# The output layer of the Hyena filters: two fp32 matmuls over 64 rows, or single passes with a low part in the other 64 rows

## The chip, the cores and the metric

The kernel runs on one core of a Trainium2 chip. Its time is device microseconds for one execution; the median of three runs counts. Beside these times there is one profiled execution, from which every line of the profile below is taken. PE is the matmul engine (its weight loads are listed apart, as PEld), DVE the vector engine, ACT the scalar engine, POOL the GpSimd engine, SP the engine whose queue issues most of the transfers (DMA).

## The reference, cut to what matters

The program is one layer of a bidirectional encoder over 2048 positions of width 1024: an input projection, a Hyena group (long convolutions by FFT), an mLSTM group, an output projection, cross-attention and an MLP. The change lies in the Hyena group's filters. They are generated, not stored: a small network with two sine layers of 64 units runs over position features, a linear output layer makes 2048 channels of it (2 orders x 2 directions x 512), a window damps them, and the spectrum is taken.

```
z = concat([t, cos(bands * ang), -sin(bands * ang)])          # (2048, 33)
hid = sin(fr1 * (z @ w1 + b1))                                # (2048, 64)
hid = sin(fr2 * (hid @ w2 + b2))
filt = (hid @ w3).reshape(L, 2, 2, 512)                       # order, direction, channel
filt = filt * exp(-t * abs(deltas))
two_sided = concat([filt[:, :, 0], 0, flip(filt[1:, :, 1])])
spec = rfft(two_sided)
```

Everything is fp32, and the result is held to it.

## The kernel before

The whole layer is one stream of instructions per engine. Python generators emit the work; `weave` interleaves two of them in the ratio of the weights that it is given, by the numbers that they yield. `filters()` (L158) is woven with the first sweeps of the input projection: `weave(p.filters(), s, 230, 200)` (L1621). The tile framework then orders the instructions of each engine with a timeline simulation of its own (`schedule_with_timeline_sim`, L1581, the planner in what follows), inserts the waits, and gives out buffers: a tile of a given tag takes one of that tag's `bufs` slots and waits until the tile that had it is done with. An engine then takes its queue strictly in that order; an instruction that waits holds up all behind it.

`filters()` has three parts.

The sine layers (L201 to L213) make `hid`, 128 rows x 2048 positions: the upper 64 rows are the hidden units at position t, the lower 64 the same units at the mirrored position, for the backward direction. The weights `w1` and `w2` hold two copies on the diagonal, so one matmul serves both directions. They, the biases and the output weights `w3` come over POOL's queue (L175 to L187) at the very start of the program, beside the loads of x and of the projection's weights over SP's queue.

The taps loop (L244 to L263) runs over 16 residues j of the position modulo 16 (two per iteration, `j2` and `jj`) and two orders o. Each of these 32 steps multiplies every 16th column of `hid` by `w3`: L253 takes the upper 64 rows (forward), L254 the lower 64 (backward), each one fp32 matmul, which the profile shows as two records. DVE multiplies both by the window (L256, L257), adds them (L261), POOL subtracts them (L262). One step late, `front` (L235) multiplies sum and difference by the 128 x 128 matrix `f1` (L238, fp32), ACT copies the result into the tile `st` (L239), and after the second residue SP stores it to `fs` in memory (L241). A window tile holds two residues of one direction (512 KB); `windows` (L219) loads the next two ahead.

The blocks loop (L265 to L286) runs over 32 blocks, 16 for each order: SP loads a block of `fs` (L270) and two matrices `dm` (L268), PE multiplies (L284, fp32, two matmuls), ACT copies (L285), SP stores to `hd` (L286). `hyena()` reads `hd` later: L663 and L664, each a half of 64 rows, every half loaded to two places. The loads run two blocks ahead.

All tiles of the three parts come from one pool, `f_sb`: seven tiles of tag `a` (128 x 2 x 512, 512 KB), used for windows, `st`, and the loads and results of the blocks loop, and eight of tag `b` (128 x 512).

In the projection's sweeps (L295 to L297), a product of two fp32 operands is already made of three single passes in the type fp32r: each operand is split into a rounded high part (ACT, L300) and the remainder (DVE, L301), and high x high, low x high and high x low are summed. `natural()` (L593) makes the projection's columns that aren't convolved; its result goes through a tile `so` (L614) to memory, beside `st` tiles of a tag with three buffers that `prep_norm` and `sweep_out` use.

Of the kernel before, what the change touches and what calls it, by code (L numbers as in the profile page):

```python
# [18 lines left out]
L = 2048  # L19
D = 1024  # L20
CH = 512
# [6 lines left out]
def shape_constants():  # L28
# [13 lines left out]
    winb = win[back].copy()  # L42
    winb[0] = 0.0
    c_win = np.stack([win, winb], 0)

# [22 lines left out]
    dm = np.zeros((32, 2, 64, 2, 64))  # L68
# [29 lines left out]
class Prog:  # L98
# [59 lines left out]
    def filters(self):  # L158
        nc, tc, a = self.nc, self.tc, self.a
        sd = [self.dram(f"fs{o}", (2, 128, 16, CH)) for o in range(2)]  # L160
        hd = self.dram("hd", (2, 32, 128, CH))
        with tc.tile_pool(name="f_sb", bufs=1, side="right") as sb:
            def ta(bufs=7):
                return sb.tile([128, 2, CH], F32, tag="a", name="a", bufs=bufs)

            def tb(bufs=8):
                return sb.tile([128, CH], F32, tag="b", name="b", bufs=bufs)

            w1 = sb.tile([66, 128], F32, name="w1")
            w2 = sb.tile([128, 128], F32, name="w2")  # L170
            w3 = sb.tile([128, 2, CH], F32, name="w3")
            f1 = sb.tile([128, 2, 128], F32, name="f1")
            nc.vector.memset(w1, 0.0)
            nc.vector.memset(w2, 0.0)
            nc.gpsimd.dma_start(out=w1[0:33, 0:64], in_=a["hy_filt_w1"][0])  # L175
# [8 lines left out]
            w3v = a["hy_filt_w3"][0].rearrange("k (o r c) -> r k o c", o=2, r=2)  # L184
            for h in range(2):
                nc.gpsimd.dma_start(out=w3[64 * h:64 * h + 64], in_=w3v[h])
            nc.gpsimd.dma_start(out=f1, in_=a["c_f1"])  # L187
# [12 lines left out]

            hid = sb.tile([128, L], F32, name="hid")  # L201
# [12 lines left out]

            skip, skip2 = tb(), tb()
            for o, t in enumerate((skip, skip2)):
                nc.scalar.dma_start(out=t[0:1], in_=a["hy_skip"][:, o])
            wv = a["c_win"].rearrange("r (q j) c -> r q j c", j=16)
            def windows(j2):  # L219
                if j2 == 8:  # L220
                    return None
                w = ta(), ta()
                for r in range(2):
                    nc.sync.dma_start(out=w[r], in_=wv[r, :, 2 * j2:2 * j2 + 2])
                return w
# [17 lines left out]
            nxt = windows(0)  # L243
            for j2 in range(8):  # L244
                js = slice(2 * j2, 2 * j2 + 2)
                yield 14
                (wf, wb), nxt = nxt, windows(j2 + 1)
                for o in range(2):
                    st = [ta() for p in range(2)]
                    for jj in range(2):  # L250
                        j = 2 * j2 + jj
                        pf, pb = self.hy(), self.hy()
                        nc.tensor.matmul(pf, hid[0:64, j::16], w3[0:64, o], start=True, stop=True)  # L253
                        nc.tensor.matmul(pb, hid[64:128, j::16], w3[64:128, o], start=True, stop=True)  # L254
                        f, b = tb(), tb()
                        nc.vector.tensor_tensor(f, pf, wf[:, jj], ALU.mult)  # L256
                        nc.vector.tensor_tensor(b, pb, wb[:, jj], ALU.mult)  # L257
                        if j == 0:
                            nc.vector.tensor_tensor(f[0:1], f[0:1], (skip, skip2)[o][0:1], ALU.add)
                        e = [tb() for p in range(2)]  # L260
                        nc.vector.tensor_tensor(e[0], f, b, ALU.add)  # L261
                        nc.gpsimd.tensor_tensor(e[1], f, b, ALU.subtract)  # L262
                        late(lambda e=e, st=st, jj=jj, o=o, js=js: front(e, st, jj, o, js))  # L263
            late(None)
            def blocks(o, i):  # L265
                p, k = divmod(2 * i, 16)
                dm = sb.tile([128, 2, 128], F32, tag="dm", name="dm", bufs=3)
                nc.sync.dma_start(out=dm, in_=a["c_dm"][:, 2 * i:2 * i + 2])  # L268
                t = ta()
                nc.sync.dma_start(out=t, in_=sd[o][p, 8 * k:8 * k + 16].rearrange("(k r) j c -> (r j) k c", k=2))  # L270
                return dm, t
# [3 lines left out]
            for n, (o, i) in enumerate(order):  # L275
                if True:
                    yield 3.4
                    dm, t = q.pop(0)
                    if n + 2 < 32:
                        q.append(blocks(*order[n + 2]))  # L280
                    hs = ta()
                    for m in range(2):
                        pp = self.hy()
                        nc.tensor.matmul(pp, dm[:, m], t[:, m], start=True, stop=True)  # L284
                        nc.scalar.copy(hs[:, m], pp)  # L285
                    nc.sync.dma_start(out=hd[o, 2 * i:2 * i + 2].rearrange("k l c -> l k c"), in_=hs)  # L286

# [305 lines left out]
    def natural(self, hf, tiles, after=None):  # L593
# [3 lines left out]
        for c2 in tiles:  # L597
# [3 lines left out]
            for t in range(8):  # L601
# [24 lines left out]
    def hyena(self, es):  # L626
        nc, tc, a = self.nc, self.tc, self.a
        hy = self.dram("hy", (3, L, CH)).rearrange("s (q j) c -> s q j c", j=16)
        hd = self.dram("hd", (2, 32, 128, CH))
        yh = self.dram("yh", (L, CH)).rearrange("(q j) c -> q j c", j=16)  # L630
# [22 lines left out]
        def load2(o, i):  # L653
# [6 lines left out]
            nc.sync.dma_start(out=t, in_=sds[o][p, 8 * k:8 * k + 16].rearrange("(k r) j c -> (r j) k c", k=2))  # L660
            src = hd[o, 2 * i:2 * i + 2].rearrange("k (r l) c -> r l k c", r=2)
            for h in range(2):
                nc.sync.dma_start(out=hr[64 * h:64 * h + 64], in_=src[0])  # L663
                nc.sync.dma_start(out=hi[64 * h:64 * h + 64], in_=src[1])  # L664
            if i == 0:
                nc.sync.dma_start(out=hr[64:65, 0], in_=hd[o, 0, 64:65])
                nc.vector.memset(hi[0:1, 0], 0.0)
                nc.vector.memset(hi[64:65, 0], 0.0)
# [943 lines left out]
def program(p):  # L1612
    with ExitStack() as ms:
        with ExitStack() as es:
# [5 lines left out]
            next(s)  # L1620
            weave(p.filters(), s, 230, 200)  # L1621
            p.flush()
# [53 lines left out]
```

## Time and profile before

| | us |
|---|---|
| median of three runs | 3380.28 |
| the three runs | 3380.11, 3380.28, 3384.89 |
| the profiled execution | 3389.34 |
| its span | 3387.6 |
| PE busy in the span | 3200.0 |
| DVE, ACT, POOL busy | 2084.2, 1459.1, 1227.3 |

The table is read as follows. The span is the stretch between the first and the last instruction on the chip; the execution's own time has 1.7 us around it. Busy time of PE counts a matmul from its start to its modelled end, and matmuls overlap, so the distance from one start to the next is the better price. A line of the profile names the source line, engine, operation, output tile and input tiles; `x64` is the number of instructions, three numbers with slashes are the shortest, median and longest duration in ns, and brackets hold the idle time ahead of an instruction and what ended it. On the timeline, the first number is the start and the second the duration, in us.

The filters' parts are found by the first and last starts of their lines: the sine layers' first matmul (L208) is at 29.8, the last sine (L199) at 110.4; the taps loop's matmuls (L253) run from 112.9 to 300.9, the last `front` to 309.6; the blocks loop (L284) from 313.9 to 461.5.

### The profile page before, as it was taken

Reading aid. Unit: us, or ns where it says so; the run is one execution under the profiler, and the core shown is the slowest. Engines: PE = TensorE matmul, PEld = TensorE weight load, DVE = VectorE, ACT = ScalarE, POOL = GpSimd, SP = SyncE. Lnnn points to the kernel's source line nnn. Section 1 sums busy time; section 2 is a strip of 40 time slices with the busy share of each in tenths; the row PEclk is TensorE's granted clock in tenths of the full one; section 3 lists DMA queues with packets and bytes.
Section 4 is the critical chain, followed back from the end, with each engine's and each line's share of the span. In section 5 each row is a group of like instructions: output and inputs, shape, how many; then the busy total and the mean of one; then the engine's idle time right before and its main releaser. Section 6 shows DMA issues by size and latency. Waiting matters only on the chain.

```text
span 3387.6 us, 46777 instructions
## 1 busy us (share of the span) xinstructions
PE 3200.0 (94%) x15671; PEld 2560.6 (76%) x15671; DVE 2084.2 (62%) x3855; ACT 1459.1 (43%) x2771; POOL 1227.3 (36%) x862
## 2 busy tenths in 40 slices
PE   6999999899899988799999999999999999999997
PEld 5656666577676877688897987788788887888876
DVE  7584324443556757787776554765854576556695
ACT  4344434442554233344344444555655543333335
POOL 2131001210122312333325012876766564434482
PEclk9999999899999989899999999999999999999998
DMA  5356888996999578856547444765654475444424
GB/s 164 115 205 206 277 288 232 258 322 254 253 242 296 178 236 277 256 162 215 187 152 265 144 134 155 224 206 184 199 171 157 148 242 174 128 140 140 128 94 159
DMA packets 480750, 674.55 MB, mean 199 GB/s; under 512 B 41739, under 2 KB 256849, under 8 KB 479485
## 3 DMA queue, kind: packets, MB, share of 16 engines
q1 hardware_dynamic: 478904, 668.70, 62.4%
q0 software_dynamic: 1600, 2.86, 0.3%
q8 instruction: 124, 2.03, 0.2%
q14 instruction: 118, 0.96, 0.1%
q10 hardware_dynamic: 4, 0.00, 0.0%
HBM read 452.23 MB, written 219.18 MB: 198 GB/s over the span
## 4 chain that ended last, share of the span: by engine, by line
PE 47%; DVE 7%; DMA 6%; issue 2%; ACT 1%; POOL 1%; SPq 0%; DVEq 0%; ACTq 0%; POOLq 0%
PE mm L297 10%; PE mm L295 10%; PE mm L296 10%; PE hy L297 5%; PE hy L296 5%; PE hy L295 5%; DVE rw L945 1%; DVE wl L301 1%; DMA rw<-rows 1%; DMA wr<-xs 1%; DVE bl L1266 1%; PE hy L1092 1%; DMA wn<-in_xa_wq_dram 1%; DMA wr<-in_ff_w_dram 0%; PE hy L972 0%
## 5 line engine op out<-in xcount | busy, mean ns | idle before, releaser
L301 DVE TENSOR_TENSOR wl<-wn,wh 128x512 fp32r<-128x512 f32 (+1 forms) x352 | 263.1, 778 | 135.0 <-ACT wh L300 134.4
L295 PE MATMUL mm<-xh,wh 128*128 128x512 f32 (+1 forms) x768 | 316.7, 413 | 10.9 <-ACT P L530 9.3
L1266 DVE TENSOR_TENSOR bl<-wr,bh 128x512 fp32r<-128x512 f32 x213 | 237.0, 1118 | 133.2 <-ACT bh L1265 131.2
L297 PE MATMUL mm<-xh,wl 128*128 128x512 f32 (+1 forms) x768 | 302.8, 395 | 3.3 <-DVE wl L301 3.3
L1265 ACT CAST ah<-w 128x512 fp32r<-128x512 f32 x284 | 176.2, 622 | 299.9 <-PE hy L296 153.7
L296 PE MATMUL mm<-xl,wh 128*128 128x512 f32 (+1 forms) x768 | 303.7, 396 | 0.2 <-DVE xr_y L150 0.2
L300 ACT CAST wh<-wn 128x512 fp32r<-128x512 f32 (+1 forms) x352 | 202.0, 618 | 229.9 <-PE mm L296 77.1
L727 POOL TENSOR_TENSOR b<-b,a 128x512 f32<-128x512 f32 x64 | 91.9, 1438 | 498.1 <-ACT b L725 201.1
L1266 DVE TENSOR_TENSOR al<-w,ah 128x512 fp32r<-128x512 f32 x236 | 224.4, 952 | 56.8 <-ACT ah L1265 56.5
L1265 ACT CAST bh<-wr 128x512 fp32r<-128x512 f32 x232 | 143.5, 621 | 241.6 <-PE mm L297 171.1
L297 PE MATMUL mm<-bh,al 128*128 128x512 f32 x576 | 225.5, 394 | 6.6 <-DVE al L1266 3.8
L295 PE MATMUL mm<-bh,ah 128*128 128x512 f32 x576 | 227.1, 394 | 0.3 <-DVE u L1391 0.2
L296 PE MATMUL mm<-bl,ah 128*128 128x512 f32 x576 | 225.8, 392 | 0.0
L295 PE MATMUL mm<-act,wh 128*128 128x512 f32 x512 | 202.0, 398 | 6.2 <-ACT wh L300 6.2
L296 PE MATMUL mm<-act,wh 128*128 128x512 f32 x512 | 202.6, 396 | 0.0
L297 PE MATMUL mm<-act,wl 128*128 128x512 f32 x512 | 201.1, 397 | 0.0
L295 PEld LDWEIGHTS mm<-xh,wh 128*128 128x128 f32 x768 | 148.2, 193 | 60.0 <-issue 18.2
L1131 POOL TENSOR_TENSOR ssum<-ssum,sq 128x512 f32<-128x512 f32 x56 | 81.3, 1451 | 284.7 <-ACT sq L1130 283.9
L297 PEld LDWEIGHTS mm<-xh,wl 128*128 128x128 f32 x768 | 147.8, 192 | 46.3 <-issue 15.8
L296 PEld LDWEIGHTS mm<-xl,wh 128*128 128x128 f32 x768 | 147.9, 193 | 45.5 <-issue 20.0
L295 PE MATMUL hy<-bh,ah 128*128 128x512 f32 x448 | 175.2, 391 | 0.0
L296 PE MATMUL hy<-bl,ah 128*128 128x512 f32 x448 | 174.6, 390 | 0.0
(373 smaller groups left out, 8911.9 us busy)
## 6 DMA issues: line engine op xcount, KB each, us to landing
wr<-hc SPq DMA_DIRECT2D x224, 256.0 KB
w<-in_ff_w_dram SPq DMA_DIRECT2D x176, 256.0 KB
a<-hd SPq DMA_DIRECT2D x128, 256.0 KB
hc<-t SPq DMA_DIRECT2D x128, 256.0 KB
wn<-in_w_in_dram SPq DMA_DIRECT2D x104, 256.0 KB
hc<-q SPq DMA_DIRECT2D x96, 256.0 KB
fs<-a SPq DMA_DIRECT2D x32, 512.0 KB
a<-fs SPq DMA_DIRECT2D x32, 512.0 KB
```

The costliest lines, as they stand in the source:

```text
L295: mm(ps, lh, rh, start=start, stop=False)
L296: mm(ps, lh, rl, start=False, stop=False)
L297: mm(ps, ll, rh, start=False, stop=stop)
L300: self.nc.scalar.copy(hi, src)
L301: self.nc.vector.tensor_tensor(lo, src, hi.bitcast(F32), ALU.subtract)
L727: nc.gpsimd.tensor_tensor(xt, xt, hi[:, m], ALU.mult)
L945: nc.vector.scalar_tensor_tensor(nm[:, h], nm[:, h], GC[:, r + h:r + h + 1], masks[d], ALU.add, ALU.min)
L1092: nc.tensor.transpose(pt[:, 128 * k:128 * k + 128], yn[:, 128 * k:128 * k + 128], self.ident)
L1131: nc.gpsimd.tensor_tensor(ssum, ssum, sq, ALU.add)
L1265: self.nc.scalar.copy(hi, src)
L1266: eng.tensor_tensor(lo, src, hi.bitcast(F32), ALU.subtract)
```

## The change

The output layer's two 64-row fp32 matmuls of a step become four single passes in fp32r. For each direction r there is now a tile `hid[r]` with the high part of that direction's hidden units in its own 64 rows and their low part (the remainder) in the other 64, and a tile `wide[r]` with the high part of the direction's w3 in both halves. One full pass over 128 rows sums high x high and low x high; a second pass over the 64 own rows adds the high part of hid times the low part of w3 (`wl`). The splits are made where the operands are: of w3 at the start of the program, of hid after each chunk of the second sine layer.

The windows are laid out so that one tile holds both directions of one residue; the loop runs over single residues, with `st` for two of them. POOL's difference is written over `b`. There are six tiles of tag `a` and six of `b`; `w1` and `w2` lie in one of them. The blocks loop gets a pool of its own, `f_sb2`, opened when the first is closed. `hd` is stored with the two matrices of a block side by side, 4 KB in a row for 2 KB. `natural` takes its result tile from the tag `st`. The weights that the generator yields, and that of the weave, are changed with it (14 for two residues becomes 5.3 for one; 230 becomes 202).

```diff
-    c_win = np.stack([win, winb], 0)
+    c_win = np.stack([win.reshape(128, 16, CH), winb.reshape(128, 16, CH)], 2)
...
-            def ta(bufs=7):
-                return sb.tile([128, 2, CH], F32, tag="a", name="a", bufs=bufs)
-            def tb(bufs=8):
-                return sb.tile([128, CH], F32, tag="b", name="b", bufs=bufs)
-            w1 = sb.tile([66, 128], F32, name="w1")
-            w2 = sb.tile([128, 128], F32, name="w2")
-            w3 = sb.tile([128, 2, CH], F32, name="w3")
+            def ta():
+                return sb.tile([128, 2, CH], F32, tag="a", name="a", bufs=6)
+            def tb():
+                return sb.tile([128, CH], F32, tag="b", name="b", bufs=6)
+            ws = ta()
+            w1, w2 = ws[0:66, 0, 0:128], ws[:, 1, 0:128]
...
-            for h in range(2):
-                nc.gpsimd.dma_start(out=w3[64 * h:64 * h + 64], in_=w3v[h])
+            top, low = slice(0, 64), slice(64, 128)
+            wide = []
+            wl = sb.tile([128, 2, CH], F32R, name="w3l")
+            for r, own in enumerate((top, low)):
+                raw = ta()
+                for half in (top, low):
+                    nc.gpsimd.dma_start(out=raw[half], in_=w3v[r])
+                w = sb.tile([128, 2, CH], F32R, name=f"w3h{r}")
+                for o in range(2):
+                    nc.scalar.copy(w[:, o], raw[:, o])
+                    nc.vector.tensor_tensor(wl[own, o], raw[own, o], w[own, o].bitcast(F32), ALU.subtract)
+                wide.append(w)
...
-                sine(hid[:, cs], p2, 2, 3)
+                out = tb()
+                sine(out, p2, 2, 3)
+                for r, (own, other) in enumerate(((top, low), (low, top))):
+                    nc.scalar.copy(hid[r][own, cs], out[own])
+                    nc.vector.tensor_tensor(out[own], out[own], hid[r][own, cs].bitcast(F32), ALU.subtract)
+                    nc.scalar.copy(hid[r][other, cs], out[own])
...
+            for j in range(16):
+                jj = j % 2
+                js = slice(j - jj, j - jj + 2)
+                yield 5.3
+                cur, nxt = nxt, windows(j + 1)
+                if jj == 0:
+                    st = [[ta() for p in range(2)] for o in range(2)]
                 for o in range(2):
...
-                        pf, pb = self.hy(), self.hy()
-                        nc.tensor.matmul(pf, hid[0:64, j::16], w3[0:64, o], start=True, stop=True)
-                        nc.tensor.matmul(pb, hid[64:128, j::16], w3[64:128, o], start=True, stop=True)
+                    for r, own in enumerate((top, low)):
+                        p = self.hy()
+                        nc.tensor.matmul(p, hid[r][:, j::16], wide[r][:, o], start=True, stop=False)
+                        nc.tensor.matmul(p, hid[r][own, j::16], wl[own, o], start=False, stop=True)
+                        t = tb()
+                        nc.vector.tensor_tensor(t, p, cur[:, r], ALU.mult)
+                        taps.append(t)
...
             late(None)
+        with tc.tile_pool(name="f_sb2", bufs=1, side="right") as sb:
             def blocks(o, i):
...
-                t = ta()
+                t = sb.tile([128, 2, CH], F32, tag="a", name="a", bufs=8)
...
-                    nc.sync.dma_start(out=hd[o, 2 * i:2 * i + 2].rearrange("k l c -> l k c"), in_=hs)
+                nc.sync.dma_start(out=hd[o, i], in_=hs)
...
-                so = sb.tile([128, 256], F32, tag="so", name="so", bufs=3)
+                so = sb.tile([128, 512], F32, tag="st", name="st", bufs=3)[:, 0:256]
...
-            weave(p.filters(), s, 230, 200)
+            weave(p.filters(), s, 202, 200)
```

More of the change, by code (lines that the diff above doesn't have):

```diff
@@ L199, in sine @@
                 nc.scalar.activation(dst, u, AF.Sin)
-            hid = sb.tile([128, L], F32, name="hid")
+            hid = [sb.tile([128, L], F32R, name=f"hid{r}") for r in range(2)]
             for c in range(4):
@@ L212, in filters, with windows @@
                 nc.tensor.matmul(p2, w2, hid1, start=True, stop=True)
[L213 to L224 removed]
+                out = tb()
[4 more added lines that the diff above has]
+                    nc.scalar.copy(hid[r][other, cs], out[own])
+            def windows(j):
+                if j == 16:
+                    return None
+                w = ta()
+                nc.sync.dma_start(out=w, in_=a["c_win"][:, j])
                 return w
@@ L275, in filters @@
             for n, (o, i) in enumerate(order):
[L276 to L285, printed above, removed]
-                    nc.sync.dma_start(out=hd[o, 2 * i:2 * i + 2].rearrange("k l c -> l k c"), in_=hs)
+                yield 3.4
+                dm, t = q.pop(0)
+                if n + 2 < 32:
+                    q.append(blocks(*order[n + 2]))
+                hs = sb.tile([128, 2, CH], F32, tag="a", name="a", bufs=8)
+                for m in range(2):
+                    pp = self.hy()
+                    nc.tensor.matmul(pp, dm[:, m], t[:, m], start=True, stop=True)
+                    nc.scalar.copy(hs[:, m], pp)
+                nc.sync.dma_start(out=hd[o, i], in_=hs)
     def column(self, ap, n, name):
```

38 lines of the change are left out of this document (16 added, 22 removed).

## The prediction

> **What bounds the kernel now.** I read the head of the page first, then the table of windows over the stages that the change touches (the sine layers to 112 us, the taps loop from 112 to 305, the blocks loop from 313 to 465), then the timelines inside them.
>
> ```profile
> span 3387.6 us, 46777 instructions
> PE 3200.0 (94%) x15671; PEld 2560.6 (76%) x15671; DVE 2084.2 (62%) x3855; ACT 1459.1 (43%) x2771; POOL 1227.3 (36%) x862
> 0.00:60.00 60.00, 33.20 (x133) 25.32 (x134) 41.20 (x154) 27.84 (x62) 17.66 (x31) 0.97 0.72 203
> 60.00:112.00 52.00, 51.96 (x241) 41.08 (x241) 38.91 (x66) 20.33 (x32) 0.00 (x0) 1.00 0.27 76
> 112.00:305.00 193.00, 191.19 (x654) 110.16 (x653) 138.41 (x274) 77.37 (x147) 57.41 (x32) 1.00 0.49 169
> 313.00:465.00 152.00, 149.90 (x586) 102.55 (x585) 36.02 (x53) 64.92 (x111) 0.00 (x0) 0.99 0.85 284
> ```
>
> The columns of a window are its length, then busy time of PE, PE's weight loads, DVE, ACT and POOL, the granted clock, the DMA share and GB/s. From 60 us on, PE has no free time: 51.96 of 52, 191.19 of 193. Only the first 60 us have a hole (PE 33.2), and there DVE is the busiest engine (41.2). So a microsecond of PE work saved in the taps loop is a microsecond saved, and one lost in the startup is lost. Busy time overstates pipelined matmuls, so I price PE by start to start in the timeline of one step of the taps loop:
>
> ```profile
> 204.97 0.40 PE L297 MATMUL mm<-xh,wl 128*128 128x512 f32 x1
> 205.21 0.40 PE L295 MATMUL mm<-xh,wh 128*128 128x512 f32 x1
> 205.45 0.40 PE L296 MATMUL mm<-xl,wh 128*128 128x512 f32 x1
> 205.77 0.29 PEld L253 LDWEIGHTS hy<-w,hid 64*128 64x128 f32 x1 [0.37 <-issue]
> 205.77 0.80 PE L253 MATMUL hy<-w,hid 64*128 64x512 f32 x1
> 205.78 0.80 PE L254 MATMUL hy<-w,hid 64*128 64x512 f32 x1
> 206.41 0.59 PE L253 MATMUL hy<-w,hid 64*128 64x512 f32 x1
> 206.94 0.19 PEld L297 LDWEIGHTS mm<-xh,wl 128*128 128x128 f32 x1 [0.65 <-issue]
> 206.94 0.51 PE L297 MATMUL mm<-xh,wl 128*128 128x512 f32 x1
> 207.28 1.02 PE L238 MATMUL hy<-b,f 128*128 128x512 f32 x2
> ```
>
> A single 128-row pass takes 0.23 us (the three first lines). The taps product is two fp32 matmuls over 64 rows, two passes each; L253 and L254 here start together and share the array. From 205.45 to 207.28 is 1.83 us; less the two single passes in it (L296, L297, 0.46) the pair costs **1.37**. Streaming is 2 x 0.43 of that; the other 0.51 is going to 64 rows and back: 0.09 before the weight load, 0.21 in which the first load isn't hidden, 0.10 until the next 128-row load, 0.11 in which that one isn't hidden. A 64-row matmul that stands alone (159.62 to 161.45) costs the same 1.37. In the timeline 17 of the 32 steps run their two together, 15 apart (one record is missing, counted apart): 17 x 1.37 + 15 x 2.74 = **64.4 us**. As a check on the whole window: 264 sweep passes x 0.23, 60 front matmuls x 0.86 (L238, 128-row fp32: 207.28 to 208.37 less one single pass), 142 transposes x 0.115, and 64.4, make 193.0 of 193.
>
> **The taps product.** Each step now has four passes: a full one (128 rows, the high part of hid against the doubled w3) and a half one (64 rows, the low part of w3), twice, alternating. The nearest rows for the half pass are the 64-row excursions above; no row shows a 64-row single pass. By them a half pass is 0.09 + 0.21 + 0.23 + 0.10 = 0.63. The full pass's weights are every 16th column of hid, whose load takes 0.29 as at 205.77, so the first costs 0.29, the second, behind a half pass, 0.23 + 0.21 = 0.44, and the exit 0.11. A step: 0.29 + 0.63 + 0.44 + 0.63 + 0.11 = 2.10, times 32 = 67.2, against 64.4: **+2.8**. Below, if the switch costs nothing for single passes, 4 x 0.23 x 32 = 29.4, a gain of 35. Above, if a half pass streams at the fp32 pass's 0.43, 64 x (0.29 + 0.94) = 78.7, a loss of 14. I take +3, since L253 is the same operands at the same place and differs only in the type.
>
> The Trainium skill ("TensorE: Matmul & The Clock Gate", Why this matters for your kernels) says that a small-K matmul alone takes the same time as one of K=128; by that the stage would fall to 29.4, the rival below. The trace disagrees: 1.37 at 64 rows stands against 0.86 at 128. "TensorEngine Tiling (Array Packing)", Key Properties, names a cause, "Changing tiling mode (not just tile) drains the TensorE", which would be paid twice as often as now.
>
> DVE keeps its two products and the sum (0.69 each, L256, L257, L261), POOL its difference (1.78); DVE has 138 of 193, so neither bounds. The tiles f, b, e still recur every second step (4 in 8 before, 3 in 6 now): 0. The window loads stay 512 KB with 4 KB runs: 0.
>
> **Splitting hid** adds per chunk four ACT copies (0.6) and two DVE subtractions (0.69): 16 and 8, 9.6 and 5.5 us. They fall before 112, where ACT has 20 of 52 and DVE 39 of 52 busy and PE is full of sweep matmuls; that covers them. If the sweep's own DVE work gets behind, at most the 5.5. I take **+1**.
>
> **Splitting w3** stands at the start of the program, where nothing covers: four ACT casts (L300, 0.6: 2.4), four DVE subtractions (0.69: 2.7), and four loads of 256 KB on POOL's queue for two.
>
> ```profile
> 14.09 0.63 ACT L406 ACTIVATE junk<-xn 128x512 f32<-128x512 f32 x1 [1.90 <-DMA xn<-in_x_dram]
> 15.32 0.56 ACT L300 CAST xh<-mm 128x512 fp32r<-128x512 f32 x1
> 11.43 7.51 SPq L224 DMA_DIRECT2D a<-in_c_win_dram  x4
> 19.43 2.15 SPq L268 DMA_DIRECT2D dm<-in_c_dm_dram  x3
> 22.23 1.50 SPq L398 DMA_DIRECT2D xn<-in_x_dram  x2
> 23.09 0.61 POOL L186 DMA_DIRECT2D w<-in_hy_filt_w_dram  x1 [0.99 <-DMA par<-in_hy_filt_b_dram]
> ```
>
> The second w3 load is issued at 23.09 and lands 7.7 to 8.2 later, at 31; two more behind it (0.6 to 1.0 apart) land by 33, f1 by 35 instead of 32, still long before its use at 119. Each engine takes its queue in the planner's order, and the planner expects transfers sooner than they come: ACT idles for x tiles (3.77, then 1.90) while the cast of the first transposes waits behind (15.32, for transposes begun at 10.2). A w3 cast put ahead of the x work would stop ACT until 30 to 33, and the subtraction DVE, with casts, norms and the weights' splits behind them, and PE behind those. Bounds: fully in ACT's and DVE's gaps, 0; stopped from 17 to 32, **15**. The other way: only two window loads (512 KB each) are issued early for four, and the three dm loads go, so the x loads behind them on SP (22.23, landed 34.1, for which ACT waited 4.11) come some 4 us earlier, worth at most 4. DVE runs without a gap from 35.5 to 51, so the 2.7 show. 2.7 + a stop of 4 - 2.5 for earlier x: **+4**. Merging the two memsets saves 0.17 of DVE, nothing.
>
> **The pool in two.** The first blocks' dm and t take space of the first pool, whose st tiles must first be stored.
>
> ```profile
> 309.66 1.54 SPq L241 DMA_DIRECT2D fs<-a  x2
> L270 SPq DMA_DIRECT2D a<-fs x32: 360/460/1176, 301.5 to 447.5; - x32
> L284 PE MATMUL hy<-a,dm x128: 590/592/1057, 313.9 to 461.5; 128*128 128x512 f32 x128
> ```
>
> Now three t loads go out at 301.5, before the last store (issued at 310.9), and the first block multiplies at 313.9. Then loads start when that store has landed. At the 300 GB/s of these windows two 512 KB stores and the load behind them are some 5 us each, an estimate: first block at about 321, 7 late. PE has sweep work for it (73 of 165 units of the weave are left by the weights), unless the planner puts the block on PE early, or the waiting loads on SP's queue ahead of the sweep's wn loads and hy stores. Between 0 and 7: **+3**.
>
> **The rest.** hd with 4 KB runs: the half reads of hyena (L663, L664, 64 partitions) go at 143 to 250 GB/s with the DMA share over 1.0 (578 to 585 us), but the 2 KB runs of fs have reached 390, so run length isn't their limit: 0. If it is, the gain is at most the PE idle of 540 to 740, 21 us. The natural tiles' so shares st: ACT already waits 18.5 us for its stores (five times); four mm banks let PE run ahead; 0 to +5, I take 0. Weave weights (230 to 202) only move order.
>
> **Sum:** 3 + 1 + 4 + 3 = +11. The profiled execution took 3389.34 (span 3387.6, 1.7 around it), giving 3400; it is 9 above the median of the runs, 3380.28, so for the median **3391**.
>
> **Rivals.** *Passes at full rate*: the mode switch vanishes for single passes. For: weight loads are hidden in every 128-row stream. Against: every 64-row row pays 0.51. Taps -35 instead of +3: 11 - 38 = -27, 3353; half the switch paid, about 3372. It decides for faster once a half pass is under about 0.45. *Startup stopped*: w3 casts early in ACT's order, 15 for 4: +22, 3402. For: the x waits above; against: no such stop in the trace. It decides by whether the first w3 cast stands before the x work of 17 to 30 us. *Nothing shows*: sweep work covers the late blocks, the earlier x loads pay the splits, the taps come out even: 3380, within 7 either way.
>
> **Numbers.** Forecast 0.45 (own range 3384 to 3398), startup stopped 0.15, nothing shows 0.20, full rate 0.20. A measurement tells about 0.2%, 6.8 us, from none. Faster 0.21 (full rate, a sliver of even), same 0.21, slower 0.58 (forecast bar its lowest edge, and startup). The range leaves out the pure full rate and the worst stop: 3360 to 3404.
>
> **What would show it.** A half pass: 0.6 us between its neighbours, with a gap before the weight loads on either side; 0.25 refutes the taps term. Startup: PE's first full stream, now at 52 us, three to five later, and a w3 cast or subtraction waiting on its load. Blocks: first multiply 7 or so behind the last front matmul's store. Wrong most of all if the half passes run without gaps.

## The result and the profile after

The changed kernel takes 3404.9 us (median of 5, 3395.6 to 3407.9) against 3380.9 for the kernel before (median of 5, 3380.1 to 3384.9). The ratio on record is 1.0045, with a 95% interval of 1.0026 to 1.0064: slower by 15 us, between 9 and 22. The two medians lie 24 us apart, a little more than that interval allows; five runs that spread over 12 us don't settle it. The text below goes by the ratio, which low_paired (1.0044) and w3_late (1.0041), two kernels that hardly differ from the changed one, bear out. The forecast was slower, by 11 us, in a range of 3360 to 3404: 1.0045 of 3380 is 3395, within it, and the median of the five runs is 0.9 above its end. Where the forecast saw the 11 us is not where the 15 are.

The head of the page of the changed kernel, and the windows that the prediction used, in the same columns (length, busy time of PE, its weight loads, DVE, ACT and POOL, granted clock, DMA share, GB/s):

```profile
span 3406.2 us, 46844 instructions
0.00:60.00 60.00, 28.84 (x100) 21.11 (x101) 40.87 (x152) 27.65 (x61) 18.92 (x33) 0.94 0.67 179
60.00:112.00 52.00, 50.29 (x227) 39.68 (x226) 34.89 (x61) 24.96 (x40) 0.00 (x0) 0.97 0.24 69
112.00:305.00 193.00, 192.61 (x659) 122.45 (x658) 135.81 (x281) 80.77 (x152) 38.88 (x30) 0.99 0.48 166
313.00:465.00 152.00, 147.41 (x589) 101.07 (x589) 38.08 (x59) 64.31 (x110) 1.30 (x1) 1.00 0.88 303
```

In the first 60 us PE is busy for 28.8 where it was for 33.2, with 100 records where there were 133, and the granted clock is 0.94 where it was 0.97; between 60 and 112 it is 0.97 where it was 1.00. So something is lost at the start. The middle windows look alike, and their busy times tell little, because a matmul that is late or slow counts as busy too.

To see where time goes I therefore count PE's lost time: the time up to T, less what the matmuls recorded up to T need at the spacing that they have when PE is warm and fed. The prices are 0.23 us for a single pass over 512 columns, 0.43 for an fp32 pass, 0.115 for a transpose, and for the taps product what it takes in each kernel (64.4 us in all before; 0.51 a pass in the changed kernel and 0.23 where the low pass has 128 rows, both measured below). Each row comes from one profiled execution. Up to 312 us, differences of one or two us mean nothing; from 500 on, even ten may mean nothing (before_hd4, whose time is that of the kernel before, differs from it by 9 at 740). The rows below the first two are experiments of the next section.

```
lost PE time (us) up to    80    112    312    500    740    940   1160   1250
before                   35.2   35.3   31.7   36.0   64.7   80.0   87.4  112.8
after                    44.7   44.5   43.5   47.0   68.9   90.4  103.4  125.8
before_so_shared         34.4   34.3   31.7   33.9   58.0   80.1   98.0  123.7
after_so_p               44.5   44.3   40.8   42.4   67.0   85.2   94.4  118.2
before_hd4               34.7   34.3   31.6   35.7   55.2   71.4   83.9  110.7
before_two_pools         37.4   37.1   35.6   38.2   55.9   72.4   85.3  111.4
low_full_rows            44.5   44.0   53.9   55.2   75.3   97.1  109.4  141.6
low_full_so_p            41.3   41.5   51.0   53.2   68.2   83.9   97.1  129.0
w3_after_sines           35.2   34.9   45.8   47.2   68.0   84.4   98.3  130.0
```

The changed kernel loses 9.5 us by 80 us and keeps that through the taps and blocks loops. Every kernel that splits w3 at the start loses 41 to 46 by 80 us, and every one that doesn't 34 to 37, so this part is firm. Later the changed kernel gets 7 us back in the hyena stage (500 to 740) and loses 6 between 740 and 940 and 6 more by 1160, a stretch that the diff touches with one line; but kernels without that line move as much there, so these curves alone name no cause. The two profiled spans differ by 18.6 us, of which 13 stand in the table by 1250; the rest comes later and isn't followed here.

**The taps step.** PE's timeline of one step (weight loads PEld and matmuls):

```profile
208.48 0.79 PE L264 MATMUL hy<-w3h,hid 128*128 128x512 f32 x1
209.20 0.29 PEld L265 LDWEIGHTS hy<-w3l,hid 64*128 64x128 f32 x1 [0.45 <-issue]
209.20 0.60 PE L265 MATMUL hy<-w3l,hid 64*128 64x512 f32 x1
209.74 0.29 PEld L264 LDWEIGHTS hy<-w3h,hid 128*128 128x128 f32 x1 [0.25 <-issue]
209.74 0.61 PE L264 MATMUL hy<-w3h,hid 128*128 128x512 f32 x1
210.28 0.61 PE L265 MATMUL hy<-w3l,hid 64*128 64x512 f32 x1
210.82 0.51 PE L309 MATMUL mm<-xh,wh 128*128 128x512 f32 x1
211.16 0.49 PE L578 MATMUL mm<-ident,cv 128*63 128x128 f32 x3
```

From the half pass at 209.20 on, each pass starts 0.54 behind the one before, half or full, and each weight load has a gap ahead of it. The last fp32 pass of L246 ahead of the step starts at about 208.45 and takes 0.43, so 0.32 is left for the first full pass, until 209.20; the exit is 0.11 (210.82 to 211.16 less 0.23). A step is 0.32 + 3 x 0.54 + 0.11 = 2.05 us, and 32 of them 65.6. In 8 of the 32 other passes stand between the two directions, which by the same distances costs 2 x (0.32 + 0.54 + 0.11) = 1.94. So the taps product takes some 65 to 66, about 1 more than the 64.4 before.

**The start.** PE's two long stops between 30 and 50 us, where the kernel before has one (the line by itself, from its profile), and what DVE does ahead of the second in the changed kernel:

```profile
36.48 0.79 PE L309 MATMUL mm<-xh,wh 128*128 128x512 f32 x1 [6.29 <-ACT xh L314]
...
49.80 2.08 PE L220 MATMUL hy<-b,a 128*128 128x512 f32 x2 [2.89 <-ACT b L207]
```

```profile
44.77 0.67 PE L295 MATMUL mm<-xh,wh 128*128 128x512 f32 x1 [2.71 <-ACT P L530]
```

```profile
43.10 0.42 DVE L201 TENSOR_SCALAR b<-b 128x512 f32<-128x512 f32 x1
...
43.51 0.68 DVE L193 TENSOR_TENSOR w3l<-a,w3h 64x512 fp32r<-64x512 f32 x1
...
44.18 0.68 DVE L193 TENSOR_TENSOR w3l<-a,w3h 64x512 fp32r<-64x512 f32 x1
44.78 0.68 DVE L204 SCALAR_TENSOR_TENSOR b<-b 128x512 f32<-128x512 f32 x1
```

ACT's order at the start, around the first stop, and the two casts in the kernel before:

```profile
34.79 1.15 ACT L314 CAST wh<-wn 128x512 fp32r<-128x512 f32 x2 [6.54 <-DMA wn<-in_w_in_dram]
35.85 0.58 ACT L314 CAST xh<-mm 128x512 fp32r<-128x512 f32 x1
```

```profile
35.36 0.56 ACT L300 CAST xh<-mm 128x512 fp32r<-128x512 f32 x1
...
37.06 1.12 ACT L300 CAST wh<-wn 128x512 fp32r<-128x512 f32 x2
```

The x tiles do come earlier, as forecast (the last two of this group at 23.4 and 26.9, in the kernel before at 34.1 and 35.8). But then ACT stands 6.5 us for the projection's next weights, whose casts are now ahead of the cast of x (35.85) that PE needs. And the four subtractions of w3's split (the other two at 45.56 and 46.47) stand between the steps of the first sine (L201, L204, and L205 at 47.31), for whose result PE stops again.

### The profile page after: what moved, and what is told of

It reads as the page before. It is cut to its first block, busy times and chain, and to the rows that moved or that the text cites. A ratio compares the mean times of both kernels' runs of the same rounds, so it can differ in the third digit from the quotient of the medians.

```text
span 3406.2 us, 46844 instructions
## 1 busy us (share of the span) xinstructions
PE 3215.4 (94%) x15671; PEld 2582.4 (76%) x15671; DVE 2093.8 (61%) x3866; ACT 1474.3 (43%) x2793; POOL 1207.7 (35%) x864
## 4 chain that ended last, share of the span: by engine, by line
PE 47%; DVE 5%; DMA 4%; issue 1%; ACT 1%; POOL 1%; SPq 0%; ACTq 0%; DVEq 0%; POOLq 0%
PE mm L311 10%; PE mm L309 10%; PE mm L310 10%; PE hy L311 5%; PE hy L309 5%; PE hy L310 5%; DVE rw L959 1%; DMA rw<-rows 1%; DVE bl L1280 1%; DVE wl L315 1%; PE hy L1106 1%; DMA wr<-in_ff_w_dram 0%; PE hy L986 0%; DMA va<-vd 0%; DMA hg<-hg 0%
```

## The experiments

Each ratio is to runs of the kernel before on the same chip; its median there was 3394 us for the first four, 3395 for the next four, 3396 for three and 3387 for the last. 1.0045 is the changed kernel's ratio, from its own set of runs (3381 before); it was not run again beside these, so a comparison with it is one of two ratios.

### Is the switch between 64 and 128 rows the price of the half pass?

```
-  nc.tensor.matmul(p, hid[r][own, j::16], wl[own, o], start=False, stop=True)
+  nc.tensor.matmul(p, hid[r][:, j::16], wl[:, o], start=False, stop=True)
```

> The changed kernel with the low pass over all 128 rows instead of 64 (the two directions' low parts already lie in the two halves of one tile, so the pass adds low part of hid times low part of the other direction's weights, a term of the size of rounding). No pass changes between 64 and 128 rows any more. Theory (the switch is what a half pass costs): a step of the taps loop falls from 2.05 us to four passes at 0.23 to 0.29, about 1.2, so 32 x 0.85 = 27 us less, about 3378 against 3405, ratio to the kernel before 0.996 to 1.001. Rival (the taps loop isn't where time is gained, DVE or the window loads take over as the limit): the step shortens on PE but the time stays over 3395.

Ratio 0.9975 (0.996 to 0.999): 0.7% less than the changed kernel, some 24 us, and now faster than the kernel before. A step in PE's timeline:

```profile
204.78 0.80 PE L264 MATMUL hy<-w3h,hid 128*128 128x512 f32 x1
205.42 0.40 PE L265 MATMUL hy<-w3l,hid 128*128 128x512 f32 x1
205.65 0.40 PE L264 MATMUL hy<-w3h,hid 128*128 128x512 f32 x1
205.89 0.39 PE L265 MATMUL hy<-w3l,hid 128*128 128x512 f32 x1
206.12 0.39 PE L309 MATMUL mm<-xh,wh 128*128 128x512 f32 x1
```

Twice the rows, and every pass at 0.23 to 0.24, four in 0.93 us. The two excursions to 64 rows in a step of 2.05 therefore cost 1.12, or 0.56 each; the prediction had 0.51 from the fp32 rows. Of the 36 us that the taps product gives up (32 x 1.12) ten come back as lost time before 312 (43.9 at 135, 53.9 at 312); in that stretch PE now stops for 4.9 us, mostly for ACT's copies and POOL's differences, where the changed kernel has no stop.

The second edit puts both full passes ahead of both half passes in the program:

```
-  for r, own in enumerate((top, low)):
-      p = self.hy()
-      nc.tensor.matmul(p, hid[r][:, j::16], wide[r][:, o], start=True, stop=False)
-      nc.tensor.matmul(p, hid[r][own, j::16], wl[own, o], start=False, stop=True)
...
+  ps = [self.hy() for r in range(2)]
+  for r in range(2):
+      nc.tensor.matmul(ps[r], hid[r][:, j::16], wide[r][:, o], start=True, stop=False)
+  for r, own in enumerate((top, low)):
+      nc.tensor.matmul(ps[r], hid[r][own, j::16], wl[own, o], start=False, stop=True)
...
```

> The changed kernel with the order of the four passes of a step changed: both full passes first, then both half passes, whose 64-row halves can share the array. One excursion to 64 rows per step instead of two. Theory (the switch is the price): 0.29 + 0.29 + 0.09 + 0.21 + 0.23 + 0.10 + 0.11 = 1.32 per step, 32 x 0.73 = 23 us less, about 3382. Rival (each 64-row pass has its own price, its weight load that nothing hides, whatever stands beside it): 1.8 to 2.0 per step, 3400 or more.

Ratio 1.0044 (1.0029 to 1.0058): no change, but hardly a test. PE's order as it ran has 64 full and 64 half passes, and only in 7 of the 32 steps two full ones followed by two half ones; the planner sorted the others back. Such a step:

```profile
212.40 0.62 PE L264 MATMUL hy<-w3h,hid 128*128 128x512 f32 x2
212.96 0.61 PE L266 MATMUL hy<-w3l,hid 64*128 64x512 f32 x2
213.49 0.50 PE L313 MATMUL mm<-xh,wl 128*128 128x512 f32 x1
213.83 0.40 PE L311 MATMUL mm<-xh,wh 128*128 128x512 f32 x1
```

The two half passes, one in the upper and one in the lower rows, are one line here (x2): together they take 0.53, as long as one alone. The step is 1.20 us (212.40 to 213.83 less one single pass of 0.23), near the 1.32 of the theory and far from the rival's 1.8 to 2.0. So pairing saves some 0.85 us a step where it happens; 7 steps give 6 us, which the interval can't show.

### What does the tag shared by so and st cost?

The kernel before with this one line of the diff:

```
-  so = sb.tile([128, 256], F32, tag="so", name="so", bufs=3)
+  so = sb.tile([128, 512], F32, tag="st", name="st", bufs=3)[:, 0:256]
```

> The kernel before with only the result tile of the natural columns taken from the tag of the staging tiles. Theory (the shared tag costs what the changed kernel loses between 860 and 1160 us, where its lost PE time grows by 11 us more than before's): 3386 to 3392, ratio 1.002 to 1.003. Rival (that part comes from the other order of the work, not from the tag): 3381 within 3.

Ratio 1.0036 (1.0018 to 1.0054): 12 us, between 6 and 18, from a line that the prediction put at 0. The other way round, the changed kernel with so in a tile of tag P (four of them to a tile; the sweeps that use P are over by then):

```
-  so = sb.tile([128, 512], F32, tag="st", name="st", bufs=3)[:, 0:256]
+  if t % 4 == 0:
+      sot = sb.tile([128, 1042], F32, tag="P", name="so", bufs=2)
+  so = sot[:, 256 * (t % 4):256 * (t % 4) + 256]
```

> The changed kernel with the natural tiles' so taken out of tag st again: four of them share one tile of tag P, which the sweeps use and which is free by then. Theory (the shared tag costs by itself what it cost in the kernel before, 12 us, 0.36%): ratio to the kernel before 1.0045 - 0.0036 = 1.001, between 1.000 and 1.002, and PE loses 7 or 8 us between 1000 and 1160, as the kernel before does, instead of 13. Rival (the tag's cost is the planner's new order of the hyena stage and comes in any order): 1.0045 stays.

Ratio 1.0014 (0.9999 to 1.003), where 1.001 was expected. By these ratios two thirds of the slowdown is this line, some 10 us; with both intervals it is between 2 and 19. And the run is no pure way back: so in P has eight places where it had three, so the waits for so's own stores go too (ACT waits 18.5 us for `vd<-so` in the kernel before, 14.4 for `vd<-st` in the changed one, and not at all here). The clean test is the one line in the kernel before.

The step from 940 to 1160 in the table seems to show the line: 7.4 us before, 17.9 with the shared tag alone, 13.0 in the changed kernel, 9.2 with so in P. It doesn't: four kernels without the shared tag (before_hd4, before_two_pools, low_full_so_p, w3_after_sines) lose 12.5 to 13.9 there. What goes with the tag are ACT's waits for the sweeps' stores, `kn<-st`: 16 to 24 us in all in the five kernels that share it, 3 to 6 in the nine that don't. ACT's timeline of the kernel before with the shared tag, where the sweeps hand over to the natural tiles (L618 is so's line there):

```profile
1103.32 1.28 ACT L618 ACT_TABLE_LOAD   x1 [7.46 <-DMA kn<-st]
...
1113.79 0.38 ACT L618 ACTIVATE st<-mm 128x256 f32<-128x256 f32 x1 [6.19 <-DMA kn<-st]
```

and what PE waits for in that stretch:

```profile
1105.62 0.28 PE L588 MATMUL mm<-ident,cv 128*16 128x128 f32 x1 [2.73 <-DVE sg L623]
1109.64 0.40 PE L295 MATMUL mm<-wh,xh 128*128 128x272 f32 x1 [2.02 <-DVE st L142]
```

Now so needs a buffer whose store to `kn`, by the sweeps, has not landed. ACT stands 7.5 and 6.2 us, and PE stops 2.7 and 2.0 us for banks that are emptied behind those waits; from 1100 to 1120 PE loses 6.1 us where the kernel before loses 0.2. That one has a stop of 2.6 just ahead of 1100, though, and from 1060 to 1120 the difference is some 5 us. The changed kernel shows the same waits (6.2, 5.6 and 1.9 for `kn<-st`), but PE loses only some 2 us between 1100 and 1120 there, so where its ten us come out on PE stays open. In the kernel before with the shared tag about as much is lost between 1020 and 1060, 8.3 against 2.7, where PE waits twice behind casts that wait for wn loads; no st store is named there, and before_hd4, without the tag, loses some 8 us there too. So the traces tie about 5 of the 12 us to the tag; the rest rests on the ratio alone.

### What does the start cost, and by which step?

First the split of w3 put behind the sine layers in the program, the same lines moved:

> The changed kernel with the loads and the splitting of w3 moved behind the sine layers, just ahead of the taps loop. Theory (the startup loses its time to the split of w3: its 2.2 us of casts, 2.7 us of subtractions and 1 MB of loads among the first projections): the PE time lost up to 80 us falls from 44.7 to about 37, and the kernel to about 3397. Rival (the order that the planner chose for the first weights' casts, behind transfers that land late, and the split of hid): it stays at 44 and 3405 within 4.

Ratio 1.0041 (1.0014 to 1.0067), lost time at 80 us 42.5: the rival. But the edit had not reached the chip: POOL issued the four loads at 23.9 us all the same, and the subtractions ran from 43.9 to 46.8 (43.5 to 47.2 in the changed kernel): the planner had put them back among the first instructions. This run does not clear the split.

The runs that follow build on a kernel with 128-row low passes and with so in P. That kernel itself:

> Low pass over all 128 rows (its product then has a small further term of hid's low part by the other direction's low w3), and so from tag P. If the two costs are separate, the gains add: 0.9975 - 0.0036 = 0.994, about 3360 against 3381. If the shared tag is hidden in the faster kernel, 0.9975.

Ratio 0.9952 (0.9933 to 0.9972): the two gains add, within the interval. At the start it has the code and the order of the changed kernel, with much the same stop before L220 (3.17 for 2.89), yet loses 41.3 by 80 us and not 44.7: here PE is granted the full clock in 50 to 55 us, there half of it.

w3's loads and split ahead of the loads of w1 and w2 on POOL's queue:

> The kernel of the run above with the loads and the split of w3 ahead of the loads of the first two layers' weights on POOL's queue. The instruction lists show PE's second sine layer (L220) after 49 sweep passes instead of 24, and the first (L216) after 32 transposes instead of 24, both as in the kernel before. Theory (PE loses 9 us by 80 us, since the planner put the sine layers so early in PE's order that PE stands for the sine and then runs its next 8 passes at a lower clock): the wait of about 3 us before L220 goes, PE's lost time at 80 us falls from 44.5 to 36 to 39, the ratio is 0.0015 to 0.0025 lower than that of the run above. Rival (the split's ACT and DVE work is itself what delays PE): the wait moves to another instruction, the time stays within 0.1%.

Ratio 0.9964 (0.9948 to 0.9979), lost time at 80 us 42.2. PE's second layer moved as the order said, and the wait moved with it: 3.19 at 49.41, in front of transposes that wait for DVE. The theory that PE's order makes the loss fell here: its 36 to 39 did not come.

w3's four subtractions on POOL, and then hid's eight too:

```
-  nc.vector.tensor_tensor(wl[own, o], raw[own, o], w[own, o].bitcast(F32), ALU.subtract)
+  nc.gpsimd.tensor_tensor(wl[own, o], raw[own, o], w[own, o].bitcast(F32), ALU.subtract)
```

> Low pass over all 128 rows and so from tag P, as in the run of these two, with w3's four subtractions on POOL, which is idle from 30 to 112 us, instead of DVE. Theory (the startup's loss is DVE's work: stopped with ACT behind the late wn loads until 35, then full from 40 to 55, so that 2.7 us more of it come out on PE wherever PE's order puts the wait): the 3.17 before L220 falls to 1 or less, PE's lost time at 80 us from 41.3 to 37 to 39, ratio 0.9944 where the run without had 0.9952. Rival (the stop of ACT from 28 to 34.6 behind the wn loads is all of it): the wait only moves, as it did when w3 was loaded first, and the lost time at 80 us stays at 41 to 42.

> As the run above, with the eight subtractions of hid's split on POOL too. DVE then has 8 us less before 112 than in the changed kernel. If DVE bounds past 60 us as well, PE's lost time at 112 us falls by another 1 to 3 us; if sweep matmuls cover hid's split, as the prediction has it, it stays within 1 us of the run above and the time within 0.1%.

Both 0.9965 (0.9953 to 0.9978), lost time at 80 us 45.5 and 43.6; the stop before L220 is 3.55 in the first, 1.61 in the second. DVE gained nothing by it. POOL's line and DVE's of the first of these two runs:

```profile
42.47 5.64 POOL L193 TENSOR_TENSOR w3l<-a,w3h 64x512 fp32r<-64x512 f32 x4 [16.74 <-ACT w3h L192]
```

```profile
42.74 1.56 DVE L315 TENSOR_TENSOR wl<-wn,wh 128x512 fp32r<-128x512 f32 x1
44.22 1.50 DVE L201 TENSOR_SCALAR b<-b 128x512 f32<-128x512 f32 x1
45.65 1.25 DVE L155 SCALAR_TENSOR_TENSOR xr_y<-xr_t,xr_y 128x1 f32<-128x1 f32 x1
...
46.89 1.76 DVE L204 SCALAR_TENSOR_TENSOR b<-b 128x512 f32<-128x512 f32 x1
```

While POOL subtracts, DVE's instructions take 1.56 for 0.68, 1.50 for 0.42, 1.25 for 0.15 and 1.76 for 0.68: 4.1 us more, against 2.7 taken away. So this pair could not test what it was made for.

Last, w3's raw halves in tiles of tag b, which the sine layers use up to their end, so that loads and split really come behind them:

```
+  for r, own in enumerate((top, low)):
+      w = sb.tile([128, 2, CH], F32R, name=f"w3h{r}")
+      for o in range(2):
+          raw = tb()
+          for half in (top, low):
+              nc.gpsimd.dma_start(out=raw[half], in_=w3v[r, :, o])
...
```

> Low pass over all 128 rows and so from tag P, with w3's raw halves in four tiles of tag b taken after the sine layers, so that their loads wait until the last chunk's sine tiles are free. In the order of DVE the four subtractions then stand behind the sine layers, where they stood among the steps of the first sine (43.5 to 47.1 us, between L201 and L205). PE's order at the start is the same as without. Theory (these 2.7 us lie in the chain DVE sine steps, ACT sine, PE's second layer L220, and PE waits for it): the wait of 3.17 before that layer (now L211) falls to 1 or less, with it the slow passes behind it, PE's lost time at 80 us from 41.3 to 37 to 39, ratio 0.994 where the run without had 0.9952. Rival (the late casts of wn set the startup): the wait moves to another instruction and the lost time at 80 us stays at 41 or more.

Ratio 0.9931 (0.9916 to 0.9946). The loads go out at 109.7 to 119, the subtractions run at 124 to 131, and the lost time is that of the kernel before: 35.2 us at 80, where the run without has 41.3. Its first casts of wn after 22 us, and PE at the second layer (now L211), where no wait is left:

```profile
30.05 1.12 ACT L315 CAST wh<-wn 128x512 fp32r<-128x512 f32 x2
```

```profile
42.51 1.12 PE L211 MATMUL hy<-b,a 128*128 128x512 f32 x2
```

These casts run at 30.05 and not 34.79. The 1 MB of w3 (four loads of 256 KB, issued from 21.8 on in the changed kernel) is then out of the way of the wn loads issued from 23 on: between 30 and 35 us the DMA engines are busy for 0.50 of the time here and for 0.88 in the changed kernel. And the sine chain is rid of 2.7 us on DVE. So the split of w3, standing at the start, is the loss of the start. How much its loads and how much its subtractions cost is not separated: this edit moves both, and SP's queue has changed its order with it (the window loads now go ahead of the x tiles, 11.3 against 17.5; in the changed kernel the x tiles go first, at 12.2). The theory of the subtractions alone can't be all, since the wn casts came 4.7 us earlier as well. Of the 6 us some 2 are left at 620 us, and by 940 none in these two profiles. The two intervals of the ratio overlap, so a gain in time over the run without is not shown.

### The hd layout and the second pool, each alone

```
-  hd = self.dram("hd", (2, 32, 128, CH))
+  hd = self.dram("hd", (2, 16, 128, 2, CH))
...
-  nc.sync.dma_start(out=hd[o, 2 * i:2 * i + 2].rearrange("k l c -> l k c"), in_=hs)
+  nc.sync.dma_start(out=hd[o, i], in_=hs)
...
```

> The kernel before with the layout of hd alone changed (two blocks side by side, runs of 4 KB for 2 KB). Forecast: nothing, 0.999 to 1.001. Rival (the run length limits hyena's half reads): PE's idle time between 540 and 740 falls, by 7 us as the two curves of lost PE time differ there, ratio 0.998, by 21 at the most, 0.994.

Ratio 0.9994 (0.9982 to 1.0006): nothing, as forecast. Its lost time between 540 and 740 falls by 9 us, and a glance would give that to the longer runs; but the next kernel, without them, falls as much there:

```
+  with tc.tile_pool(name="f_sb2", bufs=1, side="right") as sb:
+      def ta():
+          return sb.tile([128, 2, CH], F32, tag="a", name="a", bufs=8)
...
       def blocks(o, i):
```

> The kernel before with only the second pool added: the blocks take their tiles from a pool of their own. Theory by the curves of lost PE time (flat from 312 to 500 in the changed kernel): the first block starts 7 or 8 us later behind the last front, sweep matmuls fill PE, ratio 0.999 to 1.001. Rival (the prediction's +3, up to 7 if PE waits for the block): 1.001 to 1.002, with a wait of PE for a<-fs at 315 to 325 and the lost time 3 to 7 us higher there.

Ratio 1.0009 (0.9996 to 1.0022). The first block multiplies at 323.45 and not 313.88, PE has no wait for it, and the lost time stays flat from 312 to 500 (35.6 to 38.2). In the changed kernel:

```profile
321.80 1.13 SPq L249 DMA_DIRECT2D fs<-a  x2
...
328.60 0.43 SPq L285 DMA_DIRECT2D a<-fs  x1
...
333.62 1.88 PE L298 MATMUL hy<-a,dm 128*128 128x512 f32 x4
```

The loads wait for the stores of 321.8, and the first block comes 11.8 us behind them (4.2 before): 7.6 late, where 7 was forecast.

## Why the prediction was right, and where it was wrong

- **That PE bounds** held, with one refinement: what counts is not only how long PE stops but how fast it runs afterwards (below).
- **Taps product, +3:** right by mechanism and size. Measured about +1 (65 to 66 for 64.4). A half pass is 0.54 and not 0.63, the full pass behind it 0.54 and not 0.44. That the change of rows is paid "twice as often as now" was too much: the kernel before has 43 stretches of 64-row passes in PE's order, the changed one 64. The rival of passes at full rate fell: 0.54 lies above the 0.45 at which it would have decided, and low_full_rows shows what that rate would have been worth, and that the switch takes it. By the Trainium skill's "TensorE: Matmul & The Clock Gate" (Why this matters for your kernels), where a small-K matmul takes as long as a full one, the half pass would have been 0.23; the trace has 0.54 where the passes alternate. "TensorEngine Tiling (Array Packing)" of the Trainium skill (Key Properties), which has a change of mode drain the engine, agrees with these rows.
- **Hid's split, +1:** not measured alone. With hid's subtractions on POOL or on DVE the lost time at 112 differs by 2 us, in the range of what other orders do, and POOL's work slows DVE's (below), so the run that was to show it couldn't. Nothing here contradicts +1.
- **w3's split and the start, +4 (0 to 15):** the size in the stage was 9.5, within the bounds, but the step that was to carry the upper part did not happen. The w3 casts did not stop ACT; they ran at 41.5 without a wait on their load. What stopped ACT was the next weights of the projection, which landed late beside w3's loads, and the four subtractions stood in the first sine's chain, where the forecast let them show as 2.7 at most. The earlier x tiles, counted as a gain of 2.5, came and gained nothing, because ACT then waited for the wn loads. What the 9.5 us at 80 are worth in the kernel's time is not shown: the one run that takes them away has an interval that overlaps with that of the run without. What to look for had been named (a w3 cast or subtraction that waits): it was not there.
- **The pool in two, +3:** the lateness was right (7.6 for 7). Its cost is 1.0009 alone, between -1 and +7 us; the curve up to 500 shows PE covered by sweep matmuls. Not told apart from 0 or 3.
- **hd, 0:** right.
- **so sharing st, 0 (0 to 5): the step that failed.** It costs 12 us alone (6 to 18) and, less surely, some 10 in the changed kernel. The argument was that ACT already waited 18.5 us for so's own stores and that four mm banks let PE run ahead. But so had waited for its own stores, within the natural tiles; a shared tag makes it wait for another stage's, at the hand-over, where ACT also has that stage's copies to do. The four mm banks did not let PE run past that: it stopped 2.7 and 2.0 us, for the banks of both.
- **The sum:** +11 was forecast without the shared tag. Without it the changed kernel stands at 1.0014, +5 us, between 0 and 10 (more, as far as so's eight places gain by themselves). So the sum of the other terms was probably too high, by which term stays open, and the total came near because one term of 0 was 10. That is luck: two errors of opposite sign. The direction was right for reasons that were about a third of the cause. The windows' new layout, the smaller pools and the new weights of the weave, which the prediction put at 0, were not run alone.

## What to carry to other kernels

A step down to half the rows cost nearly the same here whether the pass in it was long or short (0.51 us with fp32 passes, 0.56 with single ones); shortening the passes inside without taking away the steps buys little, and filling the unused rows can be the faster way to compute less. A buffer tag shared to save memory joins the waits of two stages: look at what is still being stored where one hands over to the other, not at how long each waits by itself. And an instruction moved in the program has not moved until the trace shows it: moving the lines left w3's split at 44 us, and only a dependency, a buffer that comes free late, held it back.

The version that follows from the runs, 128-row low passes with so in P and w3 split after the sines, takes 0.9931 of the time before (0.9916 to 0.9946) and is some 1.1% faster than the change as it was made.

## What the runs showed of the hardware that was not expected

**A stop of PE can cost more than its length.** PE's timeline in the changed kernel:

```profile
1064.22 2.05 PE L704 MATMUL hy<-b,em 128*128 128x512 f32 x2 [3.64 <-ACT P L544]
1065.28 1.42 PE L309 MATMUL mm<-xh,wh 128*128 128x512 f32 x1
1066.49 0.63 PE L310 MATMUL mm<-xl,wh 128*128 128x512 f32 x1
1066.92 0.63 PE L311 MATMUL mm<-xh,wl 128*128 128x512 f32 x1
...
1069.83 0.39 PE L309 MATMUL mm<-xh,wh 128*128 128x512 f32 x1
1070.06 0.39 PE L310 MATMUL mm<-xl,wh 128*128 128x512 f32 x1
```

After a stop of 3.64 us the single passes start 0.43 apart instead of 0.23 until 1069.5; the window 1064.2 to 1069.5 has a granted clock of 0.50. PE loses 6.1 us there, 2.5 more than it stood. "TensorE: Matmul & The Clock Gate" (What's actually happening) of the Trainium skill has the clock halved after an idle window of some 3.4 us and a busy one needed to get it back; the 0.43 agrees with a halved clock. As a threshold the 3.4 us does not hold here: a stop of 2.89 us before L220 in the changed kernel was followed by slow passes (granted 0.50 in 50 to 55 us), one of 3.17 at the same instruction in low_full_so_p by none (1.00). The same page says that the window runs free, so that it matters when a stop falls; these two fit that, though no run here varies it by itself. With a second such stretch at 66 us (0.66 in 65 to 70) the slow passes make about the 3.4 us of lost time by which the two differ at 80 us, with the same code up to there.

**POOL slows DVE.** A tiny DVE instruction of 0.15 us took 1.25 while POOL subtracted, and one of 0.42 took 1.50, so moving 2.7 us of work from DVE to an idle POOL cost DVE 4.1. The Trainium skill's "SBUF — State Buffer" (SBUF: two separate sides) gives both one shared pair of ports under an exclusive lock, which fits: each of the four took 0.9 to 1.1 us longer, not quite one of POOL's instructions (5.64 / 4 = 1.41).

**The hyena stage keeps no account.** Its lost time between 500 and 740 was 29 us before and 18 to 24 in three kernels that differ from it by one part each. In the two of them whose time is that of the kernel before, all but 2 us of the gain was gone by 1250. A gain or a loss of ten us read there from one profile says little of a part; only the ratios of whole runs did.
